# Differential attention with rope products and low parts on VectorE, two key low-part buffers, and identity products between adaLN parts

## The chip, the cores and the metric

One core of a Trainium2 chip runs the kernel. The metric is the device time of one execution in microseconds: 723.41 as the median of three runs (722.85 to 723.57).

The engines are TensorE (PE in the profile, with PEld for its weight loads), VectorE (DVE), ScalarE (ACT), GpSimd (POOL) and SyncE (SP), which here only issues transfers. Each takes the instructions of its own queue in order and waits at an instruction whose inputs, or whose output buffer, are not ready.

## The reference, cut to what matters

A backbone of two layers over 512 latent tokens and 256 context tokens of width 1024. Each layer normalises its input, scales and shifts it by adaLN terms, and runs its mixer.

```
for li in range(2):
    shift, scale, gate = split(silu(cond) @ ada_w[li] + ada_b[li], 3)     # for c and for c_ctx
    x = rms_norm(h, norm_w[li]) * (1 + scale) + shift
    h = h + gate * mixer(x)          # layer 0: A and B, layer 1: C
return rms_norm(h_lat, final_w)

# A: spatial gating      gelu(u) * (w_s . layer_norm(gelu(v)) + b_s) * silu(z)
# B: differential attention, 4 heads, keys and queries of 2 x 64
s = q . k / 8                        # q, k of the latent tokens with rope
a = softmax(s[0]) - lam * softmax(s[1])
o = rms_norm(a @ v, subln_w) * (1 - lam_init) * silu(z)
# C: latent attention, 8 heads, low-rank keys and values, one shared rope key

def apply_rope(x, cos, sin):         # rot: halves of each 32 channels exchanged, one negated
    return x * cos + rot(x) * sin
```

## The kernel before, in words

Everything is fp32. A matmul operand is split into a high part in TensorE's rounded fp32 form and a low part, the remainder (`split`, `load_w`, L62 to L71: ScalarE copies the high part, VectorE or GpSimd subtracts it, line L67), and `mm3` (L79 to L81) adds three products: high by high, high by low, low by high. In the trace `wh` and `wl` are the parts of a weight block of 128x1024, `xh` and `xl` those of activations, `ah` and `al` those of the transposed attention weights, `ks` and `kl` those of the keys. `mm`, `S` and `tr` are the PSUM buffers of projections, scores and transposes.

**The start.** After 24 products of the identity with itself (L399, they keep TensorE at work while the first data arrive), `ada_chunk(0, 0)` multiplies 32 columns of conditioning by four adaLN weight tiles of 512 KB (L174), copies the 128x128 result to SBUF (`arow`, L177), transposes it (L179), and adds biases into `AD` and `gT` (L186 to L189). `modulate_in` transposes x (L363), and scales and shifts it into `xh` (ScalarE, L366) and, by way of `xm`, into `xl` (VectorE, L368 and L371). The projections of stage A begin with these (`av_part`), each quarter of the columns with an adaLN chunk of its own. The squares of x for its norm are taken on both engines (`junk`, L221, ScalarE; `jk`, L337, VectorE).

**The other adaLN chunks.** Eight more chunks are worked off by `ada_step` in stage A and later, between projections, each with one row copy and one transpose.

**Attention B** (`diff_head`, four heads): projections of q and k, each with a weight block (`load_w`, low part on GpSimd); rope (L304 to L307: a shuffle on VectorE, the products with cos and sin on GpSimd, their sum on VectorE); `stack_q` and the keys' parts `KS` (two buffers) and `KL` (one, L535); then three pairs of query tiles. For each tile and each of the two maps: scores (L551 with `ks`, L553 with `kl`), maximum (L325), exponential with its sum (L326). Then the reciprocal of one sum (L557), its product with the other sum and `nlam` (L558, 128x1), the difference of the maps (L559), transposes of it (L569), its parts `ah` and `al` (L66, L67), and the products with the values. The values' weights (`value_columns`, two blocks a pair of heads) and the four gate weight blocks behind B also have their low parts on GpSimd.

**C** (layer 1) uses the same `rope` for four query blocks and for the shared key (`krr`).

The order of instructions on each engine is not the order of the source. A scheduler places every instruction by its own estimate of costs and of the times at which inputs and buffers become free, and `issue_after` holds some back behind a named instruction. Changing an engine or adding an instruction can thus move others.

## Time and profile before

| | |
|---|---|
| median of 3 runs | 723.41 us (722.85 to 723.57) |
| the profiled execution | 724.22 us, span 722.4 us |
| TensorE busy | 696.5 us (96%) |
| VectorE busy | 414.2 us (57%) |
| ScalarE busy | 361.0 us (50%) |
| GpSimd busy | 112.8 us (16%) |
| mean granted TensorE clock | 0.990 of full speed |
| chain that ended last | TensorE 72%, VectorE 14%, ScalarE 6%, DMA 3% |

Times in the trace are microseconds from the span's start. The span is 1.8 us shorter than the profiled execution. An identity product or an adaLN product of the program appears as two records (24 identity products are "x48"). Matmuls overlap in the array, so that the duration of one is longer than the step from one to the next. An idle time is named with the instruction that ended it. A granted clock of 1.00 is 2.4 GHz, 0.50 is 1.2 GHz; a value between is a mean over the stretch.

### The profile page before, as it was taken

How to read it: one execution, taken by the hardware profiler on the slowest of the kernel's cores; microseconds unless marked ns; L12 is line 12 of the kernel's file. 1: busy time of each engine (PE TensorE's matmuls, PEld its weight loads, DVE VectorE, ACT ScalarE, POOL GpSimd, SP SyncE). 2: the span in 40 equal slices, each digit the busy share in tenths (PEclk: the TensorE clock that was granted, in tenths of full speed). 3: DMA queues.
4: the chain of work that ended last, by engine and by line, in shares of the span. 5: the costliest groups of instructions: out<-in, count | busy, mean ns of one | idle time of the engine just before them, and what ended most of it. 6: DMA issues, size and time to landing. Idle time of an engine off the chain costs nothing.

```text
span 722.4 us, 12836 instructions
## 1 busy us (share of the span) xinstructions
PE 696.5 (96%) x5342; PEld 635.5 (88%) x5342; DVE 414.2 (57%) x765; ACT 361.0 (50%) x697; POOL 112.8 (16%) x85
## 2 busy tenths in 40 slices
...
GB/s 341 408 136 263 303 339 262 118 1 44 65 22 47 30 30 35 26 57 32 71 163 98 110 42 2 58 160 45 98 49 1 1 1 2 1 59 30 117 30 88
DMA packets 19932, 68.39 MB, mean 95 GB/s; under 512 B 3105, under 2 KB 3233, under 8 KB 19873
## 3 DMA queue, kind: packets, MB, share of 16 engines
...
q8 instruction: 42, 0.69, 0.4%
...
## 4 chain that ended last, share of the span: by engine, by line
PE 72%; DVE 14%; ACT 6%; DMA 3%; issue 2%; POOL 2%; SPq 0%; POOLq 0%; ACTq 0%
PE mm L79 16%; PE mm L80 16%; PE mm L81 16%; PE tr L174 3%; DVE s L325 3%; PE S L79 3%; PE S L81 3%; PE S L80 3%; PE tr L909 2%; ACT e L326 1%; DVE al L67 1%; PE tr L569 1%; PE S L892 1%; PE S L888 1%; PE S L553 1%
## 5 line engine op out<-in xcount | busy, mean ns | idle before, releaser
L79 PE MATMUL mm<-xh,wh 128*128 128x512 f32 (+1 forms) x240 | 84.6, 352 | 0.0
L81 PE MATMUL mm<-xh,wl 128*128 128x512 f32 (+1 forms) x240 | 84.5, 352 | 0.0
L80 PE MATMUL mm<-xl,wh 128*128 128x512 f32 (+1 forms) x240 | 84.1, 350 | 0.0
L326 ACT ACTIVATE e<-S,s 128x768 f32<-128x768 f32 (+1 forms) x80 | 65.2, 817 | 21.5 <-DVE s L325 20.9
L67 POOL TENSOR_TENSOR wl<-wr,wh 128x1024 fp32r<-128x1024 f32 (+1 forms) x20 | 47.8, 2397 | 175.2 <-ACT wh L66 117.9
L325 DVE TENSOR_REDUCE s<-S 128x1 f32<-128x768 f32 (+1 forms) x80 | 67.1, 840 | 3.7 <-PE S L892 2.4
L66 ACT ACTIVATE wh<-wr 128x1024 fp32r<-128x1024 f32 (+1 forms) x40 | 41.9, 1048 | 52.1 <-PE mm L80 19.2
L67 DVE TENSOR_TENSOR al<-tr,ah 128x512 fp32r<-128x512 f32 x76 | 49.9, 682 | 11.3 <-ACT ah L66 10.8
L66 ACT ACTIVATE ah<-tr 128x512 fp32r<-128x512 f32 x76 | 43.1, 595 | 21.6 <-PE tr L569 12.9
L79 PE MATMUL mm<-wh,xh 128*128 128x256 f32 (+1 forms) x176 | 52.2, 298 | 0.0
L80 PE MATMUL mm<-wl,xh 128*128 128x256 f32 (+1 forms) x176 | 51.7, 295 | 0.5 <-POOL wl L67 0.5
L81 PE MATMUL mm<-wh,xl 128*128 128x256 f32 (+1 forms) x176 | 51.0, 292 | 0.0
L79 PEld LDWEIGHTS mm<-xh,wh 128*128 128x128 f32 x240 | 45.2, 188 | 4.8 <-ACT wh L66 0.2
L81 PEld LDWEIGHTS mm<-xh,wl 128*128 128x128 f32 x240 | 45.2, 188 | 4.8 <-DVE wl L67 0.2
L80 PEld LDWEIGHTS mm<-xl,wh 128*128 128x128 f32 x240 | 45.2, 188 | 4.6
L67 DVE TENSOR_TENSOR wl<-wr,wh 128x1024 fp32r<-128x1024 f32 x20 | 25.0, 1250 | 28.2 <-ACT wh L66 28.2
L79 PE MATMUL mm<-wo,xh 128*128 128x256 f32 x144 | 41.0, 284 | 0.0
L80 PE MATMUL mm<-wo,xh 128*128 128x256 f32 x144 | 40.7, 283 | 0.0
L81 PE MATMUL mm<-wo,xl 128*128 128x256 f32 x144 | 40.3, 280 | 0.0
L305 POOL TENSOR_TENSOR qr<-z,cos_sb 128x512 f32<-128x512 f32 x12 | 15.6, 1296 | 158.2 <-ACT z L856 81.3
L154 POOL TENSOR_TENSOR s<-s,mhalf 128x6 f32<-128x6 f32 (+4 forms) x15 | 15.3, 1020 | 155.1 <-DVE s L227 70.6
L79 PEld LDWEIGHTS mm<-wh,xh 128*128 128x128 f32 x176 | 33.7, 192 | 1.5 <-ACT xh L366 0.6
...
## 6 DMA issues: line engine op xcount, KB each, us to landing
...
```

Of the source, the lines that this page charges most:

```text
L66: ACT.activation(h, src, AF.Copy)
L67: (eng or DVE).tensor_tensor(l, src, h.bitcast(F32), op=ALU.subtract)
L79: PE.matmul(ps, lh, rh, start=first, stop=False)
L80: PE.matmul(ps, lh, rl, start=False, stop=False)
L81: PE.matmul(ps, ll, rh, start=False, stop=last)
L154: return POOL.tensor_tensor(dst, src, mhalf[:, :n], op=ALU.pow)
L174: PE.matmul(ps[32 * b:32 * b + 32, :P], c32[:, kt, :], ws[kt // 2][:, kt % 2, b * P:(b + 1) * P], start=kt == 0, stop=kt == 7)
L305: POOL.tensor_tensor(dst, raw, cos, op=ALU.mult)
L325: DVE.tensor_reduce(nmx[:, :1], v[:, :, :w], axis=AX.XY, op=ALU.max, negate=True)
L326: ACT.activation(e.rearrange("p (c k) -> p c k", k=w), v[:, :, :w], AF.Exp, bias=nmx[:, :1], scale=1.0, accum_out=sm[:, col:col + 1])
L553: scored = PE.matmul(S[:, c, :n], QS[:, m, qs], KL[:, m, k0:k0 + n], start=False, stop=True)
L909: PE.transpose(ps[:, i * 256 + q * P:i * 256 + (q + 1) * P], es[q][:, (2 * j + i) * P:(2 * j + i + 1) * P], ident)
```

## The change

Five edits:

1. `turn_over(n)` puts n identity products into the sixth projection bank. It takes the place of the 24 at the start with 32, runs three more behind every second step of the first adaLN chunk's sum, and four behind the first two transposed halves of x.
2. The row copies of the eight later adaLN chunks (`ada_step`) run on ScalarE; the first four stay on VectorE.
3. In `rope`, the two products run on VectorE. There are eight ropes in B and five in C.
4. The low parts of 16 weight blocks in B run on VectorE: four of values, eight of queries and keys, four of gates.
5. `KL` has two buffers, taken in turn by heads, each with its two memsets.

```diff
--- before.py
+++ after.py
@@ -165,7 +165,7 @@
     def shift_of(li, kt, v):
         return AD[:, li, kt // 2, kt % 2, v:v + 1]
 
-    def ada_chunk(li, j, ws):
+    def ada_chunk(li, j, ws, between=None, copy=None):
 
 
         ps = tr_ps()
@@ -173,8 +173,13 @@
             for b in range(4):
                 PE.matmul(ps[32 * b:32 * b + 32, :P], c32[:, kt, :], ws[kt // 2][:, kt % 2, b * P:(b + 1) * P],
                           start=kt == 0, stop=kt == 7)
+            if between and kt % 2:
+                between(3)
         row = til(p_bg, [P, P], F32, "arow", 2)
-        DVE.tensor_copy(row, ps[:, :P])
+        if copy is ACT:
+            ACT.activation(row, ps[:, :P], AF.Copy)
+        else:
+            DVE.tensor_copy(row, ps[:, :P])
         ps = tr_ps()
         PE.transpose(ps[:, :P], row, ident)
         r = ps[:, :P].rearrange("p (b v) -> p b v", b=4)[:, :, :2]
@@ -202,7 +207,7 @@
 
     def ada_step():
         if ada_done[0] < 8:
-            ada_chunk(*ada_loaded[ada_done[0]])
+            ada_chunk(*ada_loaded[ada_done[0]], copy=ACT)
             ada_done[0] += 1
             ada_ahead()
 
@@ -302,8 +307,8 @@
     def rope(pl, raw, dst):
         sh = til(pl, [P, NL], F32, "sh")
         DVE.stream_shuffle(sh, raw, ROT)
-        POOL.tensor_tensor(dst, raw, cos, op=ALU.mult)
-        POOL.tensor_tensor(sh, sh, sin, op=ALU.mult)
+        DVE.tensor_tensor(dst, raw, cos, op=ALU.mult)
+        DVE.tensor_tensor(sh, sh, sin, op=ALU.mult)
         DVE.tensor_tensor(dst, dst, sh, op=ALU.add)
 
     def half(r0):
@@ -385,6 +390,11 @@
             for i in range(2):
                 modulate_in(j, v, i, *XT[j])
 
+    def turn_over(n):
+
+        for _ in range(n):
+            PE.matmul(avb[5][:, :P], ident, ident, start=True, stop=True)
+
     def av_part(j, w, ts):
         xh, xl = XT[j]
         wh, wl = w
@@ -394,13 +404,12 @@
                 mm3(avb[t], (xh[s], xl[s]), (wh[:, i, :], wl[:, i, :]), j == 0 and i == 0, j == 3 and i == 1)
 
 
-    ps = tr_ps()
-    for _ in range(24):
-        PE.matmul(ps[:, :P], ident, ident, start=True, stop=True)
+    turn_over(32)
     normalise(0, 0)
-    ada_chunk(0, 0, adaw[0])
+    ada_chunk(0, 0, adaw[0], between=turn_over)
     for i in range(2):
         h = modulate_in(0, 0, i, *XT[0])
+    turn_over(4)
     with tc.issue_after(h.ins):
         for q in range(4):
             ssq_quarter(xq[q], acc, q, 4, 1)
@@ -496,20 +505,21 @@
 
     late = []
 
-    KL = til(p_b, [P, 2, NT], F32R, "kl")
+    KLs = [til(p_b, [P, 2, NT], F32R, "kl", 2) for _ in range(2)]
     fill(p_b, "fill4", 16)
-    for m in range(2):
-        POOL.memset(KL[half(64 - 64 * m), m, :].bitcast(F32), 0.0)
+    for KL in KLs:
+        for m in range(2):
+            POOL.memset(KL[half(64 - 64 * m), m, :].bitcast(F32), 0.0)
 
     def value_columns(V, hp):
         def ev(p, ps):
             split(ps, V[0][:, 2 * p:2 * p + 2, :], V[1][:, 2 * p:2 * p + 2, :])
-        proj_tok(XT, load_w256(wch[12 + 2 * hp:14 + 2 * hp], eng=POOL), range(3), ev)
+        proj_tok(XT, load_w256(wch[12 + 2 * hp:14 + 2 * hp]), range(3), ev)
 
     def diff_head(h, V):
         qr = til(p_b, [P, NT], F32, "qr", 2)
         raw = til(sp, [P, NL], F32, "z", 2)
-        pl, pc = proj_feat(XT, load_w(wch[16 + 2 * h], eng=POOL), SPANS)
+        pl, pc = proj_feat(XT, load_w(wch[16 + 2 * h]), SPANS)
         evac = ACT.activation(raw, pl, AF.Copy, scale=0.125)
         if h == 0:
             with tc.issue_after(evac.ins):
@@ -523,11 +533,12 @@
             fill(p_b, "fill5", 112)
         kr = til(p_b, [P, NT], F32, "qr", 2)
         raw = til(sp, [P, NL], F32, "z", 2)
-        pl, pc = proj_feat(XT, load_w(wch[17 + 2 * h], eng=POOL), SPANS)
+        pl, pc = proj_feat(XT, load_w(wch[17 + 2 * h]), SPANS)
         ACT.activation(raw, pl, AF.Copy)
         ACT.activation(kr[:, NL:], pc, AF.Copy)
         rope(p_b, raw, kr[:, :NL])
         KS = til(p_b, [P, 2, NT], F32R, "ks", 2)
+        KL = KLs[h % 2]
         for m in range(2):
             a_, b_ = half(64 * m), half(64 - 64 * m)
             ACT.activation(KS[a_, m, :], kr[a_, :], AF.Copy)
@@ -630,7 +641,7 @@
         for i in range(2):
             h = 2 * hp + i
             o = ob[hp][:, i, :]
-            for (t0, n), ps in zip(SPANS, proj_feat(XT, load_w(wch[24 + h], eng=POOL), SPANS)):
+            for (t0, n), ps in zip(SPANS, proj_feat(XT, load_w(wch[24 + h]), SPANS)):
                 z = sp.tile([P, 512], F32, tag="z", name=nm("z"))
                 silu2(z[:, :n], ps)
                 s = slice(t0, t0 + n)
```

Lines after L215 stand 5 lines later in the changed kernel, those after L434 9, and those after L535 11.

**VectorE in the first adaLN chunk.** The names: `s_176` the sums of squares of x, `arow_260` and `arow_279` the row copy, `jk` squares of x, `wl_183` the first weight's low part, `xm` the modulated x. Before:

```order
L227 TENSOR_SCALAR s_176<-s_176 128x4
L177 COPY arow_260<-tr_227 128x128
L186 TENSOR_TENSOR AD<-tr_262,adab_sb 128x4
L188 TENSOR_TENSOR gT<-tr_262,adab_142 128x4
L189 TENSOR_TENSOR gT<-gT,normw_sb 128x4
L337 SCALAR_TENSOR_TENSOR jk_287,s_143<-x_95 128x256
L67 TENSOR_TENSOR wl_183<-wr_115,wh_182 128x1024
L368 TENSOR_SCALAR xm_272<-tr_267,gT,AD 128x512
L368 TENSOR_SCALAR xm_281<-tr_276,gT,AD 128x512
L371 TENSOR_TENSOR xl_41_191<-xm_272,xh_40_190 128x512
L371 TENSOR_TENSOR xl_41_191<-xm_281,xh_40_190 128x512
```

In the changed kernel:

```order
L232 TENSOR_SCALAR s_176<-s_176 128x4
L342 SCALAR_TENSOR_TENSOR jk_310,s_143<-x_95 128x256
L67 TENSOR_TENSOR wl_183<-wr_115,wh_182 128x1024
L342 SCALAR_TENSOR_TENSOR jk_314,s_143<-x_96 128x256
L342 SCALAR_TENSOR_TENSOR jk_318,s_143<-x_97 128x256
L342 SCALAR_TENSOR_TENSOR jk_322,s_143<-x_98 128x256
L182 COPY arow_279<-tr_234 128x128
L191 TENSOR_TENSOR AD<-tr_281,adab_sb 128x4
L193 TENSOR_TENSOR gT<-tr_281,adab_142 128x4
L194 TENSOR_TENSOR gT<-gT,normw_sb 128x4
L373 TENSOR_SCALAR xm_291<-tr_286,gT,AD 128x512
```

The first weight's low part and all four squares now stand ahead of the row copy and of the adaLN terms that come from it; before, one square and the low part stood behind the terms, and three squares behind the modulation of x (below the rows shown).

**TensorE in the same chunk** (`tr_198` and `S_189` take the identity products, `tr_227` and `tr_234` the sum, `ada` are the weight tiles). Before:

```order
L399 MATMUL tr_198<-ident 128x128 x24
L174 MATMUL tr_227<-ada_107,c_14_137 32x128 x8
L174 MATMUL tr_227<-ada_109,c_14_137 32x128 x8
L174 MATMUL tr_227<-ada_111,c_14_137 32x128 x8
L174 MATMUL tr_227<-ada_113,c_14_137 32x128 x8
L179 MATMUL tr_262<-ident,arow_260 128x128
L363 MATMUL tr_267<-ident,x_95 128x128 x4
```

In the changed kernel:

```order
L396 MATMUL S_189<-ident 128x128 x32
L174 MATMUL tr_234<-ada_107,c_14_137 32x128 x8
L396 MATMUL S_189<-ident 128x128 x3
L174 MATMUL tr_234<-ada_109,c_14_137 32x128 x8
L396 MATMUL S_189<-ident 128x128 x3
L174 MATMUL tr_234<-ada_111,c_14_137 32x128 x8
L396 MATMUL S_189<-ident 128x128 x3
L174 MATMUL tr_234<-ada_113,c_14_137 32x128 x8
L396 MATMUL S_189<-ident 128x128 x3
L184 MATMUL tr_281<-ident,arow_279 128x128
L368 MATMUL tr_286<-ident,x_95 128x128 x4
L368 MATMUL tr_295<-ident,x_95 128x128 x4
```

Behind each part of the adaLN products there are now three identity products; before, there were none.

**ScalarE around chunks (0,4) and (0,5) in stage A.** `vnh` are high parts of the normalised v, `gav` its normalised rows, `au` the gelu of u. Before:

```order
L463 ACTIVATE au_832<-mm_846 128x512
L66 ACTIVATE vnh_761<-gav_749 128x512
L66 ACTIVATE vnh_761<-gav_750 128x512
L66 ACTIVATE vnh_761<-gav_751 128x512
L66 ACTIVATE vnh_761<-gav_752 128x512
L463 ACTIVATE au_832<-mm_942 128x512
L66 ACTIVATE vnh_761<-gav_753 128x512
```

In the changed kernel:

```order
L472 ACTIVATE au_855<-mm_869 128x512
L66 ACTIVATE vnh_784<-gav_772 128x512
L66 ACTIVATE vnh_784<-gav_773 128x512
L180 ACTIVATE arow_952<-tr_919 128x128
L66 ACTIVATE vnh_784<-gav_774 128x512
L66 ACTIVATE vnh_784<-gav_775 128x512
L472 ACTIVATE au_855<-mm_965 128x512
L66 ACTIVATE vnh_784<-gav_776 128x512
L180 ACTIVATE arow_1048<-tr_1015 128x128
```

The row copies came into ScalarE's order, each behind a high part of the layer norm's result.

**GpSimd in B.** Before, a stretch of the first and second head (`wl` low parts, `qr` and `sh` rope products, `s` a reciprocal root):

```order
L306 TENSOR_TENSOR sh_1981<-sh_1981,sin_sb 128x512
L67 TENSOR_TENSOR wl_2073<-wr_2070,wh_2072 128x1024
L305 TENSOR_TENSOR qr_1992<-z_1993,cos_sb 128x512
L306 TENSOR_TENSOR sh_2052<-sh_2052,sin_sb 128x512
L67 TENSOR_TENSOR wl_2490<-wr_2487,wh_2489 128x1024
L67 TENSOR_TENSOR wl_2560<-wr_2557,wh_2559 128x1024
L67 TENSOR_TENSOR wl_2901<-wr_2898,wh_2900 128x1024
L305 TENSOR_TENSOR qr_2485<-z_2486,cos_sb 128x512
L306 TENSOR_TENSOR sh_2545<-sh_2545,sin_sb 128x512
L67 TENSOR_TENSOR wl_2971<-wr_2968,wh_2970 128x1024
L154 TENSOR_TENSOR s_2480<-s_2480,mhalf 128x6
L305 TENSOR_TENSOR qr_2555<-z_2556,cos_sb 128x512
```

In the changed kernel, from the last products of stage A to C:

```order
L491 TENSOR_TENSOR au_856<-au_856,z_1920 128x512
L512 MEMSET kl_1934 64x768
L512 MEMSET kl_1935 64x768 x2
L154 TENSOR_TENSOR s_2506<-s_2506,mhalf 128x6
L154 TENSOR_TENSOR s_2914<-s_2914,mhalf 128x6
L154 TENSOR_TENSOR s_3490<-s_3490,mhalf 128x6
L154 TENSOR_TENSOR s_3898<-s_3898,mhalf 128x6
L67 TENSOR_TENSOR wl_4916<-wr_4913,wh_4915 128x896
```

What stays in B is one reciprocal root a head (L154).

**VectorE in the second head.** `s_2740` is the `nlam` product that follows one reciprocal, `al` the low parts of the pair ahead, `e` the difference of the maps, `qr` and `sh` rope. Before:

```order
L559 SCALAR_TENSOR_TENSOR e_2651<-e_2652,s_2670,e_2651 128x768
L307 TENSOR_TENSOR qr_2896<-qr_2896,sh_2956 128x512
L557 RECIPROCAL s_2740<-s_2723 128x1
L325 TENSOR_REDUCE s_2752<-S_2747 128x1
L558 SCALAR_TENSOR_TENSOR s_2740<-s_2627,nlam,s_2740 128x1
L67 TENSOR_TENSOR al_2680<-tr_2674,ah_2679 128x512
L67 TENSOR_TENSOR al_2689<-tr_2683,ah_2688 128x512
L559 SCALAR_TENSOR_TENSOR e_2721<-e_2722,s_2740,e_2721 128x768
L325 TENSOR_REDUCE s_2760<-S_2755 128x1
```

In the changed kernel (`s_2766` is the same product):

```order
L311 TENSOR_TENSOR sh_2982<-sh_2982,sin_sb 128x512
L568 RECIPROCAL s_2696<-s_2679 128x1
L330 TENSOR_REDUCE s_2755<-S_2750 128x1
L569 SCALAR_TENSOR_TENSOR s_2696<-s_2653,nlam,s_2696 128x1
L330 TENSOR_REDUCE s_2763<-S_2758 128x1
L570 SCALAR_TENSOR_TENSOR e_2677<-e_2678,s_2696,e_2677 128x768
L312 TENSOR_TENSOR qr_2922<-qr_2922,sh_2982 128x512
L568 RECIPROCAL s_2766<-s_2749 128x1
L330 TENSOR_REDUCE s_2778<-S_2773 128x1
L67 TENSOR_TENSOR al_2706<-tr_2700,ah_2705 128x512
L67 TENSOR_TENSOR al_2715<-tr_2709,ah_2714 128x512
L569 SCALAR_TENSOR_TENSOR s_2766<-s_2653,nlam,s_2766 128x1
```

The two low parts `al` moved ahead of the `nlam` product, and a rope product (L311) entered the stretch.

## Rows read from the trace of the kernel before

**Rows 1.** Timeline, TensorE: start us, us, instruction, count, [idle before <- releaser].

```profile
1.57 7.05 PE L399 MATMUL tr<-ident 128*128 128x128 f32 x48 [1.57 <-POOL ident masks.py:199]
10.57 0.64 PE L174 MATMUL tr<-ada,c 128*32 128x128 f32 x16 [1.95 <-DMA ada<-in_ada]
...
14.32 1.08 PE L174 MATMUL tr<-ada,c 128*32 128x128 f32 x16 [0.20 <-DMA ada<-in_ada]
15.81 0.47 PE L179 MATMUL tr<-ident,arow 128*128 128x128 f32 x1 [0.41 <-DVE arow L177]
16.08 1.92 PE L363 MATMUL tr<-ident,x 128*128 128x128 f32 x8
18.01 1.22 PE L79 MATMUL mm<-wh,xh 128*128 128x512 f32 x2
```

**Rows 2.** Windows: each engine busy, PEclk, DMA share, GB/s.

```profile
12.00:20.00 8.00, 7.17 (x62) 4.96 (x55) 3.93 (x10) 5.12 (x14) 0.00 (x0) 0.50 1.03 400
20.00:22.00 2.00, 2.00 (x7) 1.55 (x6) 1.91 (x8) 2.00 (x8) 0.00 (x0) 0.59 1.04 414
```

**Rows 3.** Timeline of VectorE, 14 to 22 us.

```profile
15.47 0.29 DVE L177 COPY arow<-tr 128x128 f32<-128x128 f32 x1 [5.03 <-PE tr L174]
...
16.67 0.42 DVE L337 SCALAR_TENSOR_TENSOR jk<-x 128x256 f32<-128x256 f32 x1
...
17.01 1.22 DVE L67 TENSOR_TENSOR wl<-wr,wh 128x1024 fp32r<-128x1024 f32 x1
```

**Rows 4.** Timeline of ScalarE, 14 to 22 us.

```profile
15.60 1.06 ACT L66 ACTIVATE wh<-wr 128x1024 fp32r<-128x1024 f32 x1 [2.28 <-DMA wr<-in_ew]
```

**Rows 5.** Waits of TensorE: us in total, times, longest us.

```profile
PE tr L569 <- DVE al L67: 3.8, 4, 1.7
...
PE S L553 <- DVE kl L535: 1.3, 2, 0.6
```

**Rows 6.** Timeline of all engines, near two adaLN chunks of stage A.

```profile
71.95 1.24 ACT L66 ACTIVATE vnh<-gav 128x512 fp32r<-128x512 f32 x2 [0.76 <-DVE gav L454]
...
80.89 0.29 DVE L177 COPY arow<-tr 128x128 f32<-128x128 f32 x1
...
81.23 0.33 PE L179 MATMUL tr<-ident,arow 128*128 128x128 f32 x1 [1.18 <-DVE arow L177]
```

**Rows 7.** Timeline of VectorE, second head of B.

```profile
243.93 2.12 DVE L558 SCALAR_TENSOR_TENSOR s<-s,nlam,s 128x1 f32<-128x1 f32 x1
245.98 1.27 DVE L67 TENSOR_TENSOR al<-tr,ah 128x512 fp32r<-128x512 f32 x2
```

**Rows 8.** Timeline of GpSimd, the same place.

```profile
243.66 2.38 POOL L67 TENSOR_TENSOR wl<-wr,wh 128x1024 fp32r<-128x1024 f32 x1 [2.99 <-ACT wh L66]
```

**Rows 9.** Windows of B: PE, PEld, DVE, ACT, POOL busy, PEclk, DMA, GB/s.

```profile
240.00:260.00 20.00, 17.51 (x118) 14.86 (x117) 19.53 (x35) 13.07 (x29) 4.33 (x3) 1.00 0.08 26
...
sum 200.00, PE 192.46 PEld 172.95 DVE 129.53 ACT 110.38 POOL 59.33; mean PE 19.25 PEld 17.29 DVE 12.95 ACT 11.04 POOL 5.93
```

**Rows 10.** Timeline of TensorE, second and fourth head of B.

```profile
246.71 0.66 PE L569 MATMUL tr<-ident,e 128*128 128x128 f32 x4 [1.67 <-DVE al L67]
...
338.32 0.65 PE L569 MATMUL tr<-ident,e 128*128 128x128 f32 x4 [1.31 <-DVE al L67]
```

**Rows 11.** Line L558: duration ns min/median/max, first and last start.

```profile
L558 DVE SCALAR_TENSOR_TENSOR s<-s,nlam,s x24: 200/210/2316, 196.9 to 349.5; 128x1 f32<-128x1 f32 x24
```

**Rows 12.** Groups by line, GpSimd and VectorE: busy us, mean ns | idle before.

```profile
L67 POOL TENSOR_TENSOR wl<-wr,wh 128x1024 fp32r<-128x1024 f32 (+1 forms) x20 | 47.8, 2397 | 175.2 <-ACT wh L66 117.9 <-DVE wo L67 57.3
...
L305 POOL TENSOR_TENSOR qr<-z,cos_sb 128x512 f32<-128x512 f32 x12 | 15.6, 1296 | 158.2 <-ACT z L856 81.3 <-DVE al L67 30.0 <-ACT z L527 23.5
...
L67 DVE TENSOR_TENSOR wl<-wr,wh 128x1024 fp32r<-128x1024 f32 x20 | 25.0, 1250 | 28.2 <-ACT wh L66 28.2
...
L558 DVE SCALAR_TENSOR_TENSOR s<-s,nlam,s 128x1 f32<-128x1 f32 x24 | 11.1, 463 | 0.0
...
L307 DVE TENSOR_TENSOR qr<-qr,sh 128x512 f32<-128x512 f32 x12 | 8.3, 689 | 13.7 <-POOL sh L306 13.7
```

## The prediction

> **What bounds the kernel now.** I read the timeline of TensorE first, then what it waited for, then the queue of the engine that came last at each wait. TensorE is busy 96% of the span, so only its idle places, and the stretches at the lower clock, have anything to give. There are three of them that the change touches.
>
> *The start.* The 24 products on the identity run from 1.57 to 8.62, and then nothing until the first adaLN weights land at 10.57 [rows 1]. The 32-column adaLN products follow in four parts, as their weights land, about 1.25 us apart (10.57 to 14.32), and end near 15.40; VectorE copies their rows at 15.47, TensorE transposes them at 15.81, transposes x from 16.08 (eight in 1.92 us) and begins the projection at 18.01. The granted clock is 0.50, which is 1.2 GHz, throughout 12 to 20 us, and 0.59 as a mean over 20 to 22 [rows 2]: it came back to 2.4 GHz near 21.6. So the projection runs for 3.6 us at half speed, a loss of 1.8 us, and has no idle time afterwards that could absorb a delay.
>
> *The adaLN chunks of stage A.* At 81.23 TensorE idles for 1.18 us behind one row copy, which stood in VectorE's queue behind layer-norm work until 80.89 [rows 6].
>
> *Attention B.* In 160 to 360 us TensorE is busy 192.46 of 200 us: 7.54 us idle [rows 9]. Half of it is transposes of the exponentials waiting for `al` (3.8 us), 1.3 the scores waiting for `kl` [rows 5]. The reason stands in two queues: VectorE's 128x1 `nlam` product takes 2.12 us at 243.93 [rows 7], beside GpSimd's weight subtraction of 243.66 to 246.04 [rows 8]; `al` follows at 245.98, and TensorE waits until 246.71 [rows 10]. The same line takes 0.21 us as a median, up to 2.32 [rows 11].
>
> **The change, part by part.** The sum is made against the profiled execution, 724.22 us, which is 0.81 above the median of 723.41; I take the difference over to the median.
>
> *1. Start.* Three things count: the dummies, the order on VectorE and the clock.
>
> The 32 dummies take 32 x 0.294 (7.05 over 24 [rows 1]) = 9.4 us and end at 10.97, so the idle 1.95 us is gone, and the first adaLN part starts 0.4 later. Each part is then 0.64 us of products (its first row, at full clock) and three dummies, 0.88: 1.52 a round, above the 1.25 at which the weights land. TensorE is continuously busy from 1.57 to about 17.05, and the adaLN sums are complete at 10.97 + 3 x 1.52 + 0.64 = 16.2.
>
> But the order on VectorE moves against it. The row copy now stands behind four squares of x and the first weight's low part, which in the kernel before stand after it. The low part needs `wh`, which ScalarE makes from 15.60 to 16.66, when its weights have landed [rows 4]. So: one square until 16.65, the low part 1.22 from 16.68 (17.90), three squares at 0.34 from start to start (16.67 to 17.01 in [rows 3]) to 18.9, the copy 0.29: 19.2 instead of 15.76, +3.4 us. TensorE, done at 17.05, then idles for about 2.1 us, in place of the 1.95 it lost at 10.57.
>
> After the copy, the kernel before needs 2.20 us from the row transpose to the projection (15.81 to 18.01), at half clock. *If the clock is still full*: 1.10, plus four dummies 1.18; start at 21.46, 3.45 later than before, of which the 1.8 us lost at half speed come back: **+1.7**. *If it fell in the pause and comes back only after 5.5 us of unbroken work* (the kernel before needs that, from 16.08 to 21.6): 2.20 + 2.36, start at 23.7; some 1.0 us at half speed costs 0.5: 5.7 + 0.5 - 1.8 = **+4.4**. I take **+3.0**, the middle: in the kernel before a pause of 1.95 us with light work behind it brought the clock down, and here the pause is as long, but heavier work surrounds it.
>
> The Trainium skill, "TensorE: Matmul & The Clock Gate", section "What's actually happening", says that the clock follows how busy TensorE has been, and calls idle the state in which it is halved. By that rule a clock kept up through the dummies would speak for +1.7, the rival named second below; no row shows such a pause after dense work.
>
> *2. Row copies on ScalarE.* ScalarE's order puts the copy of chunk (0,4) behind two layer-norm halves, which end at 73.19 [rows 6]; the chunk's products end near 72.4 and TensorE asks for the row some four products later, 72.9: a new wait of up to 0.5. The next copy stands behind one half, 0.62 us long, a wait of about 0.2. Together 0.7 instead of the 1.18 us: **-0.4**, with bounds -1.0 (both hidden by projection products) and 0. The other six copies lie in stretches where no wait for a row shows; nothing is taken for them. What hides them is TensorE's own projection work: it has other products ready while a row is copied. Should a copy fall behind a 1.06 us `wh` [rows 4], it costs at most that, once.
>
> *3. Attention B: low parts and rope on VectorE, second `kl`.* Removed from GpSimd: 16 low parts at 2.40 and 16 of its rope products at 1.30 [rows 12]. Added to VectorE: 16 x 1.25 + 16 x 0.69 [rows 12] = 31 us, in a 200 us stretch where it is busy 129.5 [rows 9], 160 afterwards. It gets back 24 x (0.46 as the mean of its `nlam` products, less 0.21 [rows 11, 12]) = 6 us, and what the `kl` and `al` subtractions lose beside GpSimd. Where does that land?
>
> The two long `al` stalls (1.67 at 246.71 and its twin of 1.31 at 338.32 in the fourth head [rows 10]) go: GpSimd now has nothing but one reciprocal root per head in this stretch, and `al` of the next pair even stands ahead of the `nlam` product. Of the 3.8 us I take all but 0.4: -3.4. The `kl` waits go with the second buffer, since the subtraction no longer waits for the last scores of the head before, nor runs beside a weight subtraction: -1.3. Of the remaining 2.4 us (`ks`, the exponentials' combination, transitions) a third goes with a free GpSimd: -0.8. Against this stands the new work in the full stretches: 240 to 260 has VectorE at 19.53 of 20 [rows 9]; one low part and two products are 2.6 us more, less the 1.9 given back by the `nlam` product: +0.7, of which TensorE, with spare projection products in the order, passes on perhaps half; twice over the two such heads, and the same once in the others: +1.0. Sum: **-4.5**, bounds -6 (nothing is passed on, one stall in five stays) and -2 (the new work eats half of it).
>
> *4. Rope in C.* The four query ropes and `krr`: shuffle, two products and a sum in one queue end about 0.15 us earlier than across two engines, and 1.4 us more work on VectorE delays the low parts behind it by 0.4 at most. No wait there names GpSimd's products. **0**, bounds +/-0.6.
>
> *5. The two extra memsets* run on GpSimd while it has nothing else to do: nothing, since no reader is near; at worst the first `kl` waits 1.5 us more, once, which the earlier free GpSimd excludes.
>
> Sum: +3.0 - 0.4 - 4.5 + 0 = **-1.9**, so 722.3 as profiled and **721.5** against the median.
>
> **The rivals.**
>
> *First, the slower one: VectorE becomes the bound in B.* Place: the scores of the second and fourth head. If the order lets two low parts and two products fall into the full stretch (3.9 us on top of 19.53, less 1.9), the stretch is 21.5 us long for VectorE, and TensorE idles 1.5 us more than its 2.5 now in the second head, keeps its stall in the fourth, and gains only the `kl` and half of the small waits: -0.5 in place of -4.5. Total +3.0 - 0.4 - 0.5 = +2.1: **725.5**. It is slower from where B gives less than 1.1 us. For it: the 19.53. Against it: this share contains the stretched operations, and the order has projection products between the scores.
>
> *Second, the clock stays at 2.4 GHz through the pause.* The start costs +1.7: total -3.2, **720.2**. For it: TensorE has no gap before 17.05. Against it: the pause is not shorter than the one of the kernel before.
>
> *Third, the clock falls at once and comes back as late as before.* The start costs +4.4, total -0.5: **722.9**, no change. For it: the fall in the kernel before, in which 1.95 us of idle time preceded it.
>
> *Fourth, the change does at the start what it says*: the copy is not held up (the low part waits, but the copy is served first). Then the projection starts at 16.2 + 0.35 + 1.10 + 1.18 = 18.8, 0.8 late, with the 1.8 us back: -1.0, total -5.9, **717.5**. Against it: VectorE takes its instructions in order, and the low part stands first.
>
> **How the numbers follow.** The forecast has 0.45 (its own range 718.5 to 724), the first rival 0.15, the second 0.15, the third 0.20, the fourth 0.05. About 0.2% (1.45 us) is what a measurement of this kernel can tell from no change: faster is below 721.96, slower above 724.86. Faster: 0.45 x 0.75 + 0.15 + 0.02 + 0.05 = 0.56; slower: 0.02 + 0.12 + 0.04 = 0.18; the rest, 0.26, is no change. The range reaches from the second rival with the better bound of B (720.2 - 1.5 - 0.5 = 718.2) to just above the first rival, 725.8; outside are most of the fourth and the corners.
>
> **What would show it.** Start: the row copy on VectorE near 19.2, behind a low part and squares; the first projection product between 21.4 and 23.8; the granted clock in 10 to 17 at 1.00, and in 19 to 24 either 1.00 or 0.50. A copy before 17 refutes the first term. Stage A: two short waits for `arow` near 73 and 82 in place of one of 1.18. B: the `nlam` products all at 0.2 us, no wait for `kl`, and TensorE's idle time in its 200 us near 3 instead of 7.5; if it is above 6.5, the first rival is right, and VectorE's busy share in the second head will be at its limit. In C nothing should move by more than 0.6. I am wrong altogether if a new wait appears in the 560 us that I have costed at nothing, above all one for VectorE where a rope product now stands ahead of a softmax row.

## The result: 716.11 us, and where it came from

The changed kernel takes 716.11 us as the median of four runs (714.93 to 716.63), against 723.41: a ratio of 0.9898, with a 95% interval of 0.9881 to 0.9915. I forecast 721.5 and a range from 718.2. The direction was right; the gain was four times what I expected, and the range missed it by two microseconds.

The span of the profiled execution fell from 722.4 to 714.3 us, by 8.1. A ledger shows where. I take instructions that both kernels have, and subtract their start times in the two timelines (a negative difference is a kernel that runs ahead of the kernel before):

| TensorE instruction | before | after | difference | the stretch to there |
|---|---|---|---|---|
| last transpose of x | 56.32 | 61.54 | +5.22 | start: +5.2 |
| first scores of B | 191.59 | 196.47 | +4.88 | stage A: -0.3 |
| first product of layer 0's output projection on B | 377.62 | 372.78 | -4.84 | B: -9.7 |
| last 256-column product of C's input projection | 472.12 | 467.27 | -4.85 | output projection, C's input: 0.0 |
| last product of the kernel | 715.02 | 706.84 | -8.18 | C and the end: -3.3 |

The start lost more than I had feared, and B and C gained more. The execution of the kernel before in this table took 724.22 us, 0.6 to 1.6 us above the medians that the ratios below are taken against (722.58 to 723.61), so that sums over the table come out larger than the differences of the medians. The page shows the sum of it: TensorE is now busy 98% of the span, with the same work and more identity products. Its row on the page of the changed kernel:

```profile
PE 697.4 (98%) x5390; PEld 641.5 (90%) x5390; DVE 432.8 (61%) x799; ACT 363.2 (51%) x705; POOL 43.4 (6%) x45
```

Of the waits of TensorE [rows 5], those for `al` and `kl` in B are gone, and so is C's wait for `al`. What is left in the changed kernel is the copy at the start, and short ones:

```profile
PE tr L184 <- DVE arow L182: 4.0, 1, 4.0
...
PE tr L775 <- DVE cql L70: 0.9, 1, 0.9
...
PE tr L597 <- ACT e L594: 0.4, 1, 0.4
PE tr L184 <- ACT arow L180: 0.4, 1, 0.4
```

**The start.** What answers to [rows 3] is VectorE's queue, with the row copy behind a low part and squares:

```profile
17.55 0.42 DVE L342 SCALAR_TENSOR_TENSOR jk<-x 128x256 f32<-128x256 f32 x1 [7.28 <-DMA x<-in_x]
...
17.90 1.22 DVE L67 TENSOR_TENSOR wl<-wr,wh 128x1024 fp32r<-128x1024 f32 x1
...
20.07 0.28 DVE L182 COPY arow<-tr 128x128 f32<-128x128 f32 x1
```

The first square waited for its part of x until 17.55, the low part started at 17.90, three more squares from 19.04 on, and the copy came at 20.07 instead of 15.47. TensorE, to be set against [rows 1], ended the last identity products at 16.43 and then waited 3.99 us:

```profile
15.49 0.94 PE L396 MATMUL S<-ident 128*128 128x128 f32 x6
20.41 0.47 PE L184 MATMUL tr<-ident,arow 128*128 128x128 f32 x1 [3.99 <-DVE arow L182]
20.68 1.92 PE L368 MATMUL tr<-ident,x 128*128 128x128 f32 x8
...
23.95 0.77 PE L79 MATMUL mm<-wh,xh 128*128 128x512 f32 x1
```

The eight transposes take 1.92 us again, which is half clock. The windows that answer to [rows 2] say the same: the clock stayed up while the identity products ran, fell in the pause (0.92 is a mean over 12 to 20 us) and was at 0.50 when the work resumed.

```profile
12.00:20.00 8.00, 4.42 (x67) 3.36 (x66) 2.45 (x8) 2.19 (x4) 0.00 (x0) 0.92 1.04 402
20.00:22.00 2.00, 1.59 (x8) 1.59 (x9) 0.75 (x6) 0.22 (x1) 0.00 (x0) 0.50 1.03 412
```

**Attention B.** From the first scores to the first transpose of stage A's output, the kernel before needs 164.7 us and the changed one 155.3. In windows cut there (start:end, then the busy time of PE, PEld, DVE, ACT and POOL), first the kernel before:

```profile
191.60:356.30 164.70, 157.16 (x1039) 139.88 (x1038) 115.25 (x202) 96.72 (x189) 46.87 (x26) 1.00 0.11 36
```

and the changed kernel, with one of its 20 us windows that have most of VectorE's work:

```profile
196.50:351.80 155.30, 154.41 (x1041) 140.26 (x1040) 124.49 (x225) 96.45 (x189) 5.37 (x3) 1.00 0.13 43
```

```profile
240.00:260.00 20.00, 19.77 (x134) 17.69 (x134) 18.91 (x36) 14.42 (x32) 0.00 (x0) 1.00 0.00 1
```

TensorE's idle time fell from 7.54 to 0.89 us. VectorE is busy for 9.2 us more and is at 18.9 of 20 us where it was at 19.5 [rows 9], and TensorE, at 19.8, doesn't wait for it. The 22 instructions that VectorE got in this stretch (10 low parts and 12 rope products) take 20.4 us together; about half of that came back, 6.1 us of it from the `nlam` products. The groups that answer to [rows 11, 12], of VectorE (L569 is the `nlam` product, L546 `kl`, L312 the sum of the rope):

```profile
L67 DVE TENSOR_TENSOR wl<-wr,wh 128x1024 fp32r<-128x1024 f32 x36 | 44.6, 1238 | 38.8 <-ACT wh L66 38.3 <-DMA absT_sb<-in_absT 0.5
...
L312 DVE TENSOR_TENSOR qr<-qr,sh 128x512 f32<-128x512 f32 x12 | 8.2, 684 | 0.1
...
L546 DVE TENSOR_TENSOR kl<-qr,ks 64x768 fp32r<-64x768 f32 x8 | 7.6, 951 | 1.4 <-ACT ks L544 1.3
...
L569 DVE SCALAR_TENSOR_TENSOR s<-s,nlam,s 128x1 f32<-128x1 f32 x24 | 5.0, 210 | 0.1
```

The `nlam` product is at 210 ns as a mean where it was at 463, and `kl` at 951 where it was at 1384 (the median of those before was 958, the longest 2111). No instruction of VectorE in B is stretched any more.

### The profile page after: what moved, and what is told of

The parts are those of the page before. It is cut to its first block, busy times and chain, and to the rows that moved or that the text cites. A ratio compares the mean times of both kernels' runs of the same rounds, so it can differ in the third digit from the quotient of the medians.

```text
span 714.3 us, 12926 instructions
## 1 busy us (share of the span) xinstructions
PE 697.4 (98%) x5390; PEld 641.5 (90%) x5390; DVE 432.8 (61%) x799; ACT 363.2 (51%) x705; POOL 43.4 (6%) x45
## 4 chain that ended last, share of the span: by engine, by line
PE 83%; DVE 7%; DMA 4%; ACT 4%; issue 1%; POOL 1%; SPq 0%; POOLq 0%; ACTq 0%
PE mm L79 18%; PE mm L81 17%; PE mm L80 17%; PE S L79 3%; PE S L80 3%; PE S L81 3%; PE tr L920 3%; PE tr L174 2%; DMA x<-in_x 2%; PE S L562 2%; PE S L564 2%; PE tr L580 2%; PE S L899 1%; PE S L903 1%; DMA wr<-in_wsT 1%
## 5 line engine op out<-in xcount | busy, mean ns | idle before, releaser
L67 DVE TENSOR_TENSOR wl<-wr,wh 128x1024 fp32r<-128x1024 f32 x36 | 44.6, 1238 | 38.8 <-ACT wh L66 38.3
L66 ACT ACTIVATE wh<-wr 128x1024 fp32r<-128x1024 f32 (+1 forms) x40 | 41.9, 1048 | 46.9 <-PE mm L80 21.4
L67 DVE TENSOR_TENSOR al<-tr,ah 128x512 fp32r<-128x512 f32 x76 | 50.3, 685 | 8.6 <-ACT ah L66 7.6
L154 POOL TENSOR_TENSOR s<-s,mhalf 128x6 f32<-128x6 f32 (+4 forms) x15 | 16.1, 1073 | 311.0 <-DVE s L602 179.5
L80 PEld LDWEIGHTS mm<-wl,xh 128*128 128x128 f32 x176 | 33.5, 190 | 1.3 <-POOL wl L67 0.7
L67 DVE TENSOR_TENSOR wo<-wr,wo 128x1024 fp32r<-128x1024 f32 x17 | 20.8, 1222 | 22.4 <-ACT wo L66 22.3
```

Of the source, the lines that this page charges most:

```text
L66: ACT.activation(h, src, AF.Copy)
L67: (eng or DVE).tensor_tensor(l, src, h.bitcast(F32), op=ALU.subtract)
L80: PE.matmul(ps, lh, rl, start=False, stop=False)
L154: return POOL.tensor_tensor(dst, src, mhalf[:, :n], op=ALU.pow)
```

## The experiments

Each run is told with its ratio to the kernel before on the same chip and its 95% interval. "B" and the like are stretches of the ledger above. Executions differ by themselves: `b_kl`, which leaves the order alone, is 1.3 us ahead in stage A, and `b_start` 1.0 us ahead in C, where nothing was changed in either. Differences of this size in the ledger are not read by themselves. A difference in a stretch is put down to an edit only where the wait behind it can be seen to go.

| kernel | ratio | start | A | B | C and the end |
|---|---|---|---|---|---|
| changed | 0.9898 | +5.2 | -0.3 | -9.7 | -3.3 |
| fix | 0.9846 | 0.0 | +0.3 | -9.4 | -3.3 |
| s_off | 0.9839 | -0.3 | +0.4 | -9.8 | -3.2 |
| b_start | 1.0045 | +4.1 | -1.2 | -0.5 | -1.0 |
| hold_read | 0.9974 | +4.1 | +1.7 | -4.8 | -3.4 |
| hold_write | 0.9920 | +5.2 | +1.5 | -9.7 | -3.6 |
| b_wl | 0.9965 | -0.2 | 0.0 | -3.3 | +0.1 |
| b_rope | 0.9959 | 0.0 | +0.2 | -2.0 | -3.0 |
| b_kl | 1.0010 | -0.2 | -1.3 | +0.7 | -0.1 |
| b_copy | 1.0017 | -0.1 | +0.8 | -0.5 | -0.2 |
| b_wlrope | 0.9853 | +0.1 | +0.2 | -9.4 | -3.0 |
| wlrope_c | 0.9838 | +0.1 | +0.2 | -9.4 | -4.5 |
| wlrope_nodum | 0.9841 | -0.3 | +0.3 | -9.8 | -3.4 |

### The start: the new one alone, taken back, and mended

`b_start` is the kernel before with the new start. `s_off` is the changed kernel with the old one:

```diff
-    turn_over(32)
+    ps = tr_ps()
+    for _ in range(24):
+        PE.matmul(ps[:, :P], ident, ident, start=True, stop=True)
     normalise(0, 0)
-    ada_chunk(0, 0, adaw[0], between=turn_over)
+    ada_chunk(0, 0, adaw[0])
     for i in range(2):
         h = modulate_in(0, 0, i, *XT[0])
-    turn_over(4)
```

> The kernel before with the new start alone. Theory: row copy near 20.1, clock at 0.50 from near 18.7 to near 25.5, and all later work 5.2 us late: 728.6. Rival (part of the delay is absorbed by later waits): 724 to 727.

> The changed kernel with the start of the kernel before: 24 identity products, none between the adaLN parts. If the start alone costs 5.2 us, as the distance between the two traces says where the first projections end (56.32 against 61.54), and the later parts do not depend on it: 716.1 - 5.2 = 710.9. Rival (the later stages gain by being late, for instance because weights have landed): 712 to 714.

Measured: `b_start` 726.54 us (1.0045, interval 1.003 to 1.006), `s_off` 711.57 us (0.9839, 0.9824 to 0.9854). The new start costs 4.1 us in the ledger of the one and 5.5 in that of the other (2.9 and 4.5 by the medians); alone it makes a kernel slower. In `b_start` the first square could start at 16.69, the copy came at 19.69, and TensorE's pause was 3.03 us. Its time lies in the rival's range: the start is 1.1 us cheaper than in the changed kernel's trace, and 1.2 and 1.0 us come back in A and C, which is no more than executions differ by there. Four traces have this start, and they fall into two pairs. `hold_read`, told below, loses 4.1 us as `b_start` does, and its clock is back at full speed at 23.0 us (23.4 in `b_start`). `hold_write` loses 5.2 as the changed kernel does, with the clock back at 26.1 (25.6). The copies lie at 19.62 to 20.07 us in all four, and that of `hold_write` (19.62) is no later than that of `hold_read` (19.67). That the later stages gain by being late is excluded by `s_off`, which has B and C as the changed kernel has them.

`fix` keeps the identity products and holds the low part and the four squares behind the adaLN terms:

```diff
-    with tc.issue_after(marks[1]):
-        ws_in = [split_w(w0)]
...
-    ada_chunk(0, 0, adaw[0], between=turn_over)
+    g0 = ada_chunk(0, 0, adaw[0], between=turn_over)
+    with tc.issue_after(g0.ins):
+        ws_in = [split_w(w0)]
...
-            ssq_vector(q, 5)
+            with tc.issue_after(g0.ins):
+                ssq_vector(q, 5)
```

> The changed kernel, with the first weight's low part and the last four squares of x held behind the adaLN terms on VectorE; the identity products stay as changed. Theory (the copy of the first adaLN row stood behind work that waits for a transfer; that pause brought the clock down): the row copy near 16.1 us instead of 20.07, no pause of TensorE over 0.5 us before 24 us, granted clock 1.00 throughout, the projection begins near 18.8 us; 5.2 us lost at the start become about 1.0 gained against the kernel before: 716.1 - 6.2 = 709.9. Rival (the clock falls by what 32-column adaLN products load it with, not by the pause): the clock falls to 0.50 between 17 and 22 all the same, and the time is 712 to 714.

Measured: 712.25 us (0.9846, 0.9827 to 0.9865). TensorE's timeline and two windows:

```profile
16.16 0.27 PE L184 MATMUL tr<-ident,arow 128*128 128x128 f32 x1
16.27 1.20 PE L368 MATMUL tr<-ident,x 128*128 128x128 f32 x8
...
18.12 0.48 PE L79 MATMUL mm<-wh,xh 128*128 128x512 f32 x1
...
20.14 0.50 PE L81 MATMUL mm<-wh,xl 128*128 128x512 f32 x1 [0.36 <-DVE xl L376]
...
23.91 0.84 PE L368 MATMUL tr<-ident,x 128*128 128x128 f32 x4 [0.24 <-ACT x L359]
```

```profile
12.00:16.00 4.00, 4.00 (x66) 3.16 (x66) 0.29 (x1) 1.75 (x5) 0.00 (x0) 1.00 1.03 399
16.00:18.00 2.00, 2.00 (x19) 1.81 (x19) 1.50 (x5) 1.57 (x3) 0.00 (x0) 1.00 1.04 392
```

The row is transposed at 16.16, without a pause, and the clock is full (eight transposes of x take 1.20 us instead of 1.92): the rival's mechanism falls, though the time lies in its range. The 5.2 us are back. But the 1.0 us more that I had counted on isn't there. At its twelfth 512-column product `fix` is 1.0 us ahead of the kernel before (21.4 against 22.4), at the 24th 0.3, at the 48th nothing (34.9 in both). ScalarE is busy 4.00 of 4 us in 26 to 30 in both, and the transposes of x at 23.91 wait for its scaling: a faster beginning only reaches that sooner.

`b_kl`, told further down, shows the same without any new start. It has the start of the kernel before in the same order, but in its trace the clock didn't fall:

```profile
12.00:20.00 8.00, 4.77 (x63) 2.94 (x55) 4.35 (x11) 5.29 (x14) 0.00 (x0) 1.00 1.03 399
```

The kernel before is at 0.50 in this window [rows 2]. Still `b_kl` is only 0.2 us ahead at the last transpose of x. TensorE waits there for `xh` (0.63 us), `xl` (0.98) and the scaled x (0.42) in turn, for which the kernel before has no such waits. In all, eight traces have this start; their clock is at half speed for 0 to 10.2 us of it, and at the last transpose of x they lie within 0.4 us of each other. So the half speed at which the kernel before begins its projection costs it 0.2 us against `b_kl`, and not the 1.8 of my prediction.

`wlrope_nodum`, told here because it belongs here, is `b_wlrope` (below) without any identity products; all else stands in the same order.

```diff
-    ps = tr_ps()
-    for _ in range(24):
-        PE.matmul(ps[:, :P], ident, ident, start=True, stop=True)
     normalise(0, 0)
```

> As the run with both moves, without any identity products at the start; the order of everything else is the same. Theory (the start is bound by the weights' transfers and ScalarE's scaling of x, which give back what a full clock gains): within 0.7 us of the run with both moves. Rival (the identity products earn the clock at which the first projection runs): 1.5 to 4 us slower.

Measured: 711.43 us (0.9841, 0.9825 to 0.9856), level with 712.16 for `b_wlrope`, whose interval overlaps. The identity products earn nothing. TensorE's timeline:

```profile
10.21 2.06 PE L174 MATMUL tr<-ada,c 128*32 128x128 f32 x28 [10.21 <-DMA ada<-in_ada]
...
12.68 1.08 PE L174 MATMUL tr<-ada,c 128*32 128x128 f32 x16 [0.20 <-DMA ada<-in_ada]
...
15.78 1.92 PE L363 MATMUL tr<-ident,x 128*128 128x128 f32 x8
...
20.03 0.51 PE L81 MATMUL mm<-wh,xl 128*128 128x512 f32 x1 [0.22 <-DVE xl L371]
```

After ten microseconds without work TensorE's first products run at half speed: a part of the adaLN sum takes 1.08 us against 0.64 in [rows 1], and the eight transposes 1.92 against 1.20 in `fix`. The windows print a clock of 1.00 for this stretch, but the trace has no record of the clock before 18.7 us, where full speed begins, and a stretch without a record is printed as 1.00. The half speed costs nothing that shows, because the projection then waits for `xl` all the same: at the last transpose of x this kernel is 0.3 us ahead of the kernel before.

### B: does GpSimd hold VectorE, or is it only slow?

My prediction gave the waits in B two causes at once. They can be told apart. GpSimd takes 2.40 us for a low part and VectorE 1.24, so the users of the result might only have waited for GpSimd. Or VectorE itself is held while GpSimd reads. `hold_read` adds to the changed kernel a subtraction on GpSimd behind each of the 16 low parts, whose result nobody reads. The order on the other four engines stays as it was. `hold_write` puts three memsets in its place, which keep GpSimd as busy and read nothing.

```diff
+    def idle_pool(raw, h):
+        POOL.tensor_tensor(raw, raw, h.bitcast(F32), op=ALU.subtract)     # hold_read
+        for _ in range(3): POOL.memset(raw, 0.0)                          # hold_write, in its place
```

> The changed kernel with 16 idle subtractions on GpSimd, one behind each low part in attention B and its gates (raw weights less their high part, into the raw weights, which nobody reads any more); the order on the four other engines is the same. Theory A (GpSimd's work with two SBUF inputs stretches VectorE's, and that made TensorE wait): VectorE's short products and subtractions beside them take up to 2.4 us, waits for al come back, plus 2 to 5 us: 718 to 721. Theory B (the waits came from the time that GpSimd itself needed, 2.40 instead of 1.24 us, before its result was there): nothing waits for the idle ones, 716.1 +/- 0.5.

> The changed kernel with three idle memsets of the raw weights on GpSimd behind each of the 16 low parts, in place of the idle subtraction of the run before: GpSimd is as busy, but reads nothing. If it is the reading that holds VectorE (theory of the Trainium skill's SBUF page, section on who interferes with whom), VectorE's short products stay at 0.21 us and the time at 716.1 +/- 0.7. If any work of GpSimd does, or if the raw buffers held longer delay the weights' transfers, 719 to 722, as with the idle subtractions (721.8).

Measured: `hold_read` 721.80 us (0.9974, 0.9963 to 0.9985), `hold_write` 717.04 (0.9920, 0.9906 to 0.9934). Theory A holds: half of B's gain (4.9 of 9.7 us) is lost to reads that nobody waits for. The time is above the range that I gave for it, because `hold_read` also loses 2.0 us against the changed kernel in stage A, which is no effect of the reads (see below). VectorE in `hold_read` (L67 is a low part, L575 the `nlam` product):

```profile
199.89 2.25 DVE L67 TENSOR_TENSOR wl<-wr,wh 128x1024 fp32r<-128x1024 f32 x1
...
218.85 2.24 DVE L575 SCALAR_TENSOR_TENSOR s<-s,nlam,s 128x1 f32<-128x1 f32 x1
```

and GpSimd at the same places:

```profile
198.64 2.41 POOL L518 TENSOR_TENSOR wr<-wr,wh 128x1024 f32<-128x1024 f32 x1 [12.65 <-DVE wl L67]
...
218.68 2.41 POOL L518 TENSOR_TENSOR wr<-wr,wh 128x1024 f32<-128x1024 f32 x1 [14.04 <-DVE s L574]
```

A low part of 1.24 us takes 2.25 and a 0.21 us product takes 2.24. The product ends with GpSimd's instruction (221.09), the low part 1.1 us behind it (202.14 against 201.05), nearly the time that it needs alone. The groups of `kl` and of the `nlam` product, `hold_read`:

```profile
L552 DVE TENSOR_TENSOR kl<-qr,ks 64x768 fp32r<-64x768 f32 x8 | 11.7, 1461 | 0.9 <-ACT ks L550 0.8
...
L575 DVE SCALAR_TENSOR_TENSOR s<-s,nlam,s 128x1 f32<-128x1 f32 x24 | 9.1, 378 | 0.1
```

and `hold_write`, with its memsets on GpSimd:

```profile
L553 DVE TENSOR_TENSOR kl<-qr,ks 64x768 fp32r<-64x768 f32 x8 | 7.6, 950 | 1.4 <-ACT ks L551 1.3
...
L576 DVE SCALAR_TENSOR_TENSOR s<-s,nlam,s 128x1 f32<-128x1 f32 x24 | 5.1, 211 | 0.1
```

```profile
L519 POOL MEMSET wr<- 128x1024 f32 x48 | 45.6, 954 | 187.9 <-DVE wl L67 127.9 <-ACT ah L66 52.0 <-issue 6.4
```

With 45.6 us of GpSimd's writing beside it, VectorE is as fast as without. The 0.9 us by which `hold_write` is behind the changed kernel lie in stage A (+1.5) and not in B. Half of that is no effect of the memsets: 1.0 us is lost near 96 us, behind one row copy on ScalarE, and the first memset starts at 133.78. For the other half, lost near 141 us, a cause isn't shown. `hold_read` loses 1.9 us at the same copy, before its first subtraction at 132.60.

The Trainium skill, "SBUF — State Buffer", section "Who interferes with whom", says that a VectorE instruction with two SBUF inputs contends with a GpSimd instruction that reads SBUF and not with one that only writes it. The two runs agree: 378 ns as the mean of the `nlam` product against 211. The same page, section "Summary: rules for kernel authors", says that the second of the two to issue blocks until the first has finished. The 2.24 us beside 2.41 bear that out: GpSimd began at 218.68 and VectorE at 218.85.

### B and C: each part alone

`b_wl` has the four edits that drop `eng=POOL`, `b_rope` the two that put rope's products on VectorE, `b_wlrope` both, and nothing else of the change.

```diff
-        POOL.tensor_tensor(dst, raw, cos, op=ALU.mult)                    # b_rope, b_wlrope
-        POOL.tensor_tensor(sh, sh, sin, op=ALU.mult)
+        DVE.tensor_tensor(dst, raw, cos, op=ALU.mult)
+        DVE.tensor_tensor(sh, sh, sin, op=ALU.mult)
...
-        pl, pc = proj_feat(XT, load_w(wch[16 + 2 * h], eng=POOL), SPANS)  # b_wl, b_wlrope, four such
+        pl, pc = proj_feat(XT, load_w(wch[16 + 2 * h]), SPANS)
```

> The kernel before with the 16 low parts of attention B on VectorE, nothing else. Theory (GpSimd's two-input work stretches VectorE's; the low parts are 38 of the 59 us of GpSimd's work in B): the two al waits of 1.67 and 1.31 us go, and those for kl shrink, since the subtraction no longer runs beside a low part: -5 to -7 in B, nothing in C: 717 to 718.5. Rival (VectorE's 20 us of added work eats its own gain as long as the rope products still run on GpSimd): -2 or less, 721.5 to 724.

> The kernel before with the 13 ropes' products on VectorE, nothing else. Theory: the 3.4 us gained in C (2.2 in its projections, 1.2 in its attention) are the ropes' alone, and in B some 2 us: 718. Rival (C gained from the other order that the whole change brought): C within 0.5 us, 721 to 723.

> The kernel before with low parts and rope products on VectorE, and nothing else of the change. Alone, the two gained 3.3 and 2.0 us in B; the changed kernel gained 9.7 there. Theory (one two-input stream on GpSimd is enough to keep most waits, and both have to go): B -9.5, C -3.2, the rest 0: 710.5 to 711.5, level with or below the changed kernel with the old start. Rival (the gains add, and the rest came from the order that copies and buffers brought): -5.3 in B, -3 in C: 715.

Measured: `b_wl` 720.36 us (0.9965, 0.9953 to 0.9976), `b_rope` 719.84 (0.9959, 0.9944 to 0.9973), `b_wlrope` 712.16 (0.9853, 0.9839 to 0.9867). In B: -3.3, -2.0, and together -9.4. Neither of my numbers for `b_wl` was right, nor for `b_rope`, whose 719.84 lies between 718 and 721; each keeps waits that the other stream still makes. In `b_rope` GpSimd's low part now stands beside the maps' difference `e`: VectorE,

```profile
211.76 2.67 DVE L559 SCALAR_TENSOR_TENSOR e<-e,s,e 128x256 f32<-128x256 f32 x1
...
214.96 1.27 DVE L67 TENSOR_TENSOR al<-tr,ah 128x512 fp32r<-128x512 f32 x2
```

GpSimd,

```profile
211.75 2.40 POOL L67 TENSOR_TENSOR wl<-wr,wh 128x1024 fp32r<-128x1024 f32 x1 [15.19 <-PE tr L569]
```

and TensorE, which waits for `al` behind it:

```profile
215.69 0.66 PE L569 MATMUL tr<-ident,e 128*128 128x128 f32 x4 [1.61 <-DVE al L67]
```

In `b_wl` it is the sine product beside an `e` of 128x256, 0.47 us at its shortest: VectorE, GpSimd and TensorE,

```profile
221.08 1.56 DVE L559 SCALAR_TENSOR_TENSOR e<-e,s,e 128x256 f32<-128x256 f32 x1
```

```profile
221.09 1.27 POOL L306 TENSOR_TENSOR sh<-sh,sin_sb 128x512 f32<-128x512 f32 x1 [0.83 <-DVE s L558]
```

```profile
222.70 0.55 PE L569 MATMUL tr<-ident,e 128*128 128x128 f32 x3 [1.15 <-DVE e L559]
```

One reading stream is enough to keep most of the cost: of the 9.4 us, 6.1 stay where the low parts alone are moved, and 7.4 where the ropes alone are. The rows show how: VectorE's chain of reciprocal, product, difference, `al` has several two-input instructions that a stream can meet. That such meetings are all of what stays isn't shown, since the scheduler's order on TensorE and VectorE is another in `b_wl` and in `b_rope`. With the order held, `hold_read` puts one stream at 4.9 us.

C's gain comes with the ropes, but not all of it is theirs. `b_rope` gains 3.0 us there, `b_wl` nothing. The rows of the kernel before that I had not looked at show how. VectorE in C, where the sum of the rope waits for GpSimd and holds all that is queued behind it:

```profile
494.88 0.69 DVE L307 TENSOR_TENSOR krr<-krr,sh 128x512 f32<-128x512 f32 x1 [1.01 <-POOL sh L306]
...
582.11 0.69 DVE L307 TENSOR_TENSOR qr<-qr,sh 128x512 f32<-128x512 f32 x1 [1.32 <-POOL sh L306]
...
585.82 1.27 DVE L67 TENSOR_TENSOR al<-tr,ah 128x512 fp32r<-128x512 f32 x2
```

and TensorE's waits there:

```profile
PE tr L909 <- DVE al L67: 1.2, 2, 0.7
...
PE S L841 <- DVE wqkl L67: 0.8, 1, 0.8
```

Both waits are still there in `b_wl` and gone in `b_rope` (`wqkl` is a low part queued behind the sum for the shared key). Together they are 2.0 us, and about that much is gained between 496 and 650 us by every kernel with the ropes on VectorE: 2.0 in `b_rope`, 2.2 in the changed kernel, and nothing in `b_wl` and `b_start`. The rest isn't the ropes'. In `b_rope` 1.5 us come in the last output products (from 677 us on), which are the same in both kernels, and where `b_kl`, without the ropes' move, also gains 0.5. In the changed kernel 1.2 come between 484 and 496 us, where `b_start` gains 1.1 with the ropes on GpSimd. That 3.0 and 3.3 are so near is chance.

`wlrope_c` is `b_wlrope` with C's low parts on VectorE too:

```diff
-        split(raw, h, l, eng=POOL)
+        split(raw, h, l)
```

> As the run with both moves, and C's four low parts of 128x896 on VectorE too. Theory: TensorE's wait of 0.45 us for GpSimd's low part near 470 us goes, and what VectorE does beside them (updates of the stream) is no longer held: -0.5 to -1 against the run with both moves. Rival: VectorE is busy with the stream's updates there, and the low part comes no earlier: 0.

Measured: 711.24 us (0.9838, 0.9825 to 0.9852) against 712.16. TensorE's wait for GpSimd near 470 us is gone, and C's input stage gains 0.5. The rest of its 1.5 us in C came in the last products, which are the same; the intervals overlap, so that more than 0.5 isn't shown. It and its equals, `s_off` and `wlrope_nodum`, are some 4.5 us faster than the changed kernel.

### The second buffer and the row copies

> The kernel before with two buffers of the keys' low part, nothing else; the order of instructions is the same on all engines but for two memsets. Theory (the second buffer lets the subtraction start before the last scores of the head before): waits for kl, 1.3 us on TensorE and 1.9 on its weight loads, go: 721.5 to 722. Rival (the subtraction is late because the keys' high part is, and because a low part on GpSimd stretches it to 2.1 us; the buffer was free long before): waits as before, 723.4.

> The kernel before with the eight later row copies of adaLN on ScalarE, nothing else. Theory: one wait of 1.18 us behind the layer norm on VectorE is exchanged for one of 0.4 to 1.0 behind the high parts on ScalarE: 722.4 to 723.2, within what can be told. Rival (copies held behind weights' high parts of 1.06 us delay later chunks): 724 or more.

`b_kl` has the second buffer alone, `b_copy` the copies on ScalarE alone, each as in the diff of the change. Measured: `b_kl` 723.50 us (1.0010, 1.0000 to 1.0020), `b_copy` 724.09 (1.0017, 1.0007 to 1.0026). The waits for `kl` in `b_kl`, and its subtraction on VectorE:

```profile
PE S L555 <- DVE kl L537: 1.3, 2, 0.6
```

```profile
L537 DVE TENSOR_TENSOR kl<-qr,ks 64x768 fp32r<-64x768 f32 x8 | 11.1, 1382 | 3.3 <-ACT ks L535 3.2
```

The wait is as before, to the tenth: the buffer was free in time. What made `kl` late was GpSimd's low part beside it, for in `b_wl`, with one buffer, the subtraction is at 950 ns and TensorE doesn't wait for `kl`. In `b_copy` one wait for VectorE's copy of 1.18 us became two for ScalarE's:

```profile
PE tr L182 <- ACT arow L178: 1.6, 2, 1.3
```

which is no gain. The longer one, 1.3 us near 91 us, stands behind a weight's high part on ScalarE that waits for its transfer. The same place in the changed kernel, where the row copy is at 95.16 and TensorE waits 0.43 us for it:

```profile
94.20 1.06 ACT L66 ACTIVATE wo<-wr 128x1024 fp32r<-128x1024 f32 x1 [1.77 <-DMA wr<-in_wsT]
```

This one wait is 0.91 us in `fix`, 1.02 in `s_off`, 1.41 in `hold_write` and 2.3 in `hold_read`, whose high part begins at 95.14 although its TensorE is 0.9 us ahead of the changed kernel's until there.

## Why the prediction failed, step by step

- **Start, +3.0.** The order was read rightly: the copy behind the low part and squares, the pause, and half clock when the work resumes. The sizes were off; the four traces with this start lose 4.1 to 5.2 us. The term that failed is the 1.8 us at half speed that I let come back. They were never lost: `b_kl` runs the same beginning at full clock and is 0.2 us ahead, since TensorE then waits for ScalarE and VectorE, where I had written that nothing could absorb a delay. Without this credit my two cases, +1.7 and +4.4, are +3.5 and +6.2, and what was measured lies between them. That the third rival's +4.4 is near the result is therefore in part luck. Smaller: I had the pause at 2.1 us, and it is 3.0 to 4.0. With the difference between 4.1 and 5.2 goes how long the clock stayed down (to 23.0 and 23.4, or to 25.6 and 26.1). It is not the square that waited for its part of x until 17.55 in the changed kernel: in `hold_write` the copy comes at 19.62, and it loses 5.2 too. The fourth rival, a copy that isn't held up, was tried as `fix`: it gains nothing at the start, where I gave it 1.0, since ScalarE's scaling of x is next.
- **Row copies, -0.4.** -0.3 in stage A in the changed kernel, but +0.3 and +0.4 in `fix` and `s_off`, where the same code runs earlier, and `b_copy` alone is no faster. The wait of 1.18 us went. Of the two waits that I put in its place, the first is 0.1 us in the changed kernel and the second isn't there; the one that came is at the third copy, 0.43 us, behind a high part of 1.06. I had named such a place, at 1.06 at most; it costs 0.4 to 2.3 us, as the high part's weight lands. That the sum came out near -0.4 is luck.
- **B, -4.5 with a bound of -6.** Measured -9.7 in the changed kernel, -9.4 for its two moves alone. The step that failed first is the new work on VectorE, for which I charged +1.0: TensorE waits for it nowhere. The second is that I summed TensorE's idle time and took that for the whole prize. My three gains were 5.5 us of idle time; 6.7 went. And TensorE's own busy time shrank by 2.75 us (157.16 to 154.41) for practically the same instructions, 1039 and 1041, a term that my sum doesn't have. The three differences, 1.0, 1.2 and 2.75, make up the miss. The products' durations, counted one by one, add up to the same (322.9 and 322.2 us); they overlap more, which fits delays too short to leave idle time between two records. Weight loads show more of each wait than products do: their idle time in this stretch fell by 9.8 us (24.82 to 15.04), which is near the whole gain. In the kernel before, those for `al` sum to 5.7 us against 3.8 [rows 5]:

```profile
PEld tr L569 <- DVE al L67: 5.7, 6, 2.1
```

- **B's reasons.** GpSimd's reads hold VectorE, as argued, and `hold_read` shows it. That the `kl` wait goes because of the second buffer is refuted; it goes because GpSimd's low part no longer runs beside the subtraction, which I had named as well.
- **C, 0.** Measured -3.3, -3.0 in `b_rope`; about 2 us of either can be put down to the ropes. The step that failed is that I put the ropes at nothing because no wait there names GpSimd's products. TensorE's waits don't, but VectorE's do, one step back: its sums wait 1.01 and 1.32 us for GpSimd, and `wqkl` and `al` are queued behind them.
- **The slower rival**, VectorE as the bound of B, is refuted: 18.9 of 20 us busy, and TensorE at 19.8. **The second rival** (the clock survives the pause) is refuted for this pause: the clock fell in all four traces. **The third** (it falls at once and comes back as late as before) named the fall rightly; the clock came back 3 to 6 us after the work resumed, at different times in the same code.
